# A second result row for each token's second expert, scatters without order, and gate/up weights read in 4 KB pieces

## The chip, the core and the metric

The kernel runs on one core of a Trainium2 chip. The metric is the device time of one execution in microseconds (us). Before the change it is 875.87 us, the median of 3 runs (875.46 to 876.12). The engines are TensorE (PE in the profile, its weight loads PEld), VectorE (DVE), ScalarE (ACT), GpSimd (POOL) and SyncE (SP), each with an in-order queue of its own. DMA engines move data between HBM and the on-chip memory; SP and POOL issue nearly all transfers here.

## The reference

One layer of a streaming encoder on 512 prompt tokens and 64 sample tokens, 576 rows of 1024 values. First comes a token mixer (sparse attention and a convolution branch), which the change does not touch. Then the part that matters:

```
h2  = x * (1 + sc2) + sh2
g   = argmax(h2 @ w_group + b_group)            # one group of four experts
top = the two best of the four experts of g;  w_top = softmax(their logits) * softmax weight of g
act = silu(gate) * up * w_top                   # gate, up = split(h2 @ w_gate_up[e])   1024 -> 2 x 256
y   = sum over the token's two experts of act @ w_down[e]                       #        256 -> 1024
x   = layer_norm(ALPHA * x + (1 + g2) * y, ln2_g, ln2_b)
```

Every token goes to exactly two of sixteen experts.

## The kernel before, in words

All 576 rows are routed first. Each expert's tokens are then gathered, pushed through the expert, and scattered back.

- `h2_d` in HBM holds the rows h2. `gather` (POOL, indirect DMA, line 1112) brings the up to 128 rows of one block into a tile `xg`, of which there are three. The work is 15 blocks: fixed experts, experts of the router's order, two heavy experts with two blocks each, and three blocks that hold two small experts of 64 rows each.
- `rows_in` (line 1127) turns a block: eight PE transposes. In each, 128 columns of `xg` are the stationary operand, and the identity moves past. The trace names the operands moving first, stationary second (`pxt<-ident,xg`).
- `gate_up` (lines 144 to 146, or 1145 for a pair) multiplies with the gate/up weights. These come in pieces of 256 rows of the 1024 x 512 matrix, four to an expert, loaded ahead by SP into a ring of 24 pieces (`load_gate_up`, line 1083). ACT and DVE split each piece into a high and a low part (lines 139 and 140). `hidden`, `turned` and `down` (lines 1150 to 1179) follow.
- `add_rows` (line 1186) scales the result on DVE, and POOL scatters it into `z_d` with an indirect DMA that adds to what is there (line 1190). A pair of small experts is scattered in two halves. `z_d` has one row for each token. It starts as the second norm's constant row (line 416, written early), and `ax_rows` (line 888) adds ALPHA * x to it by an accumulating DMA. Since both experts of a token add to one row, every scatter waits until the one before has landed.
- The block with an overflow part of a heavy expert takes its row numbers from a table in HBM: `table` scatters numbers and weights (POOL, line 1250), `place_ids` loads them back (line 1258) and DVE works out what the block needs (lines 1260 to 1262).
- After the blocks stands a loop for rows that found no place (line 1484). Its count is read at run time; here it is zero, but all engines meet at a barrier at its entry. Then five tiles of `z_d` are loaded (`zt`, line 1515), normalised (DVE lines 804, 1517, 1518; ACT lines 1505, 1507) and written out (line 1519).

In the expert part the order on PE, DVE and ACT is the order in which the code is written. POOL and SP are ordered by the scheduler.

Of the kernel before, what the change touches and what calls it, by code (L numbers as in the profile page):

```python
# [10 lines left out]
F32 = mybir.dt.float32  # L11
# [47 lines left out]
def encoder_step(ctx: ExitStack, tc: tile.TileContext, a, o):  # L59
# [3 lines left out]
    def scratch(name, shape, dt=F32):  # L63
        return nc.dram_tensor(name, shape, dt).ap()
# [4 lines left out]
    z_d = scratch("z_scr", (T, D))  # L69
# [46 lines left out]
    for j in range(2):  # L116
        G.iota(pay[:, :, j, 0], pattern=[[128, NT]], base=0, channel_multiplier=1)
# [298 lines left out]
    G.dma_start(z_d, dap(rows_d, 9 * D, [[0, T], [1, D]]))  # L416
# [394 lines left out]
    tok1 = late.tile([128, NT], F32, name="tok1", bufs=1)  # L811
    G.iota(tok1, pattern=[[128, NT]], base=1, channel_multiplier=1, allow_small_or_imprecise_dtypes=True)
# [71 lines left out]
    def ax_rows(t, behind):  # L884
        n = TS[t]
        with tc.issue_after(behind):
            (G if t > 1 else V).tensor_tensor(xn[t][0:n], xn[t][0:n], axr[0:n], op=OP.mult)
            ax_sums.append(G.dma_start(dap(z_d, t * 128 * D, [[D, n], [1, D]]), xn[t][0:n], accum_op=OP.add).ins)
# [10 lines left out]
    def route(t0, t1):  # L899
# [46 lines left out]
        V.tensor_tensor(vid, E, tok1[:, None, t0:t1, None].to_broadcast(full), op=OP.mult)  # L946
# [44 lines left out]

    ise = late.tile([128, NE], F32, name="ise", bufs=1)
    idt = late.tile([128, NE], I32, name="idt", bufs=1)
    sel = late.tile([128, 2, NE], F32, name="sel", bufs=1)

    def token_columns(src, e0, e1):
        V.tensor_scalar(ise[:, e0:e1], src, 0.0, float(OOB), op0=OP.is_equal, op1=OP.mult)
        last = V.scalar_tensor_tensor(idt[:, e0:e1], src, -1.0, ise[:, e0:e1], op0=OP.add, op1=OP.add).ins
        V.tensor_scalar(sel[:, 1, e0:e1], src, float(SEQ), None, op0=OP.is_gt)
        V.tensor_scalar(sel[:, 0, e0:e1], sel[:, 1, e0:e1], -1.0, 1.0, op0=OP.mult, op1=OP.add)  # L1000
        return last
# [67 lines left out]

    ring = []  # L1070
# [7 lines left out]
    def load_gate_up(e, c, dst, eng=SY):  # L1078
        if isinstance(e, int):
            src = dap(a["w_gate_up"], (e * D + 256 * c) * 512, [[512, 128], [128 * 512, 2], [1, 512]])  # L1080
        else:
            src = a["w_gate_up"][0, bass.ds(e, 1), 256 * c:256 * c + 256].rearrange("o (k p) n -> p (o k) n", p=128)
        return eng.dma_start(dst.rearrange("p (k n) -> p k n", k=2), src).ins
# [34 lines left out]
    def rows_in(b, whole=False):  # L1118
        x = xg[b % 3]
        xh, xl = xhl[:, b % 2, 0], xhl[:, b % 2, 1]  # L1120
        if whole:
            xwhole[b] = wp.tile([128, KT, 128], F32, name="xw", tag="whi", bufs=3)
        for q in range(2):
            pt = trp("pxt")
            for i in range(4):
                k = 4 * q + i
                PE.transpose(pt[:, 128 * i:128 * i + 128], x[:, 128 * k:128 * k + 128], ident)
            pv_ = pt.rearrange("p (k t) -> p k t", k=4)
            if whole:
# [126 lines left out]
    def place_ids(c, eng=SY):  # L1256
        ido = late.tile([128, 2], I32, name="ido", tag="ido", bufs=NPAIR)
        eng.dma_start(ido, ids_d.rearrange("(c p) d -> c p d", p=64)[bass.ds(c, 2)].rearrange("o p d -> (o p) d"))
        so = late.tile([128, 2], F32, name="so", tag="so", bufs=NPAIR)
# [3 lines left out]
        return [ido[:, 0:1]], ido.bitcast(F32)[:, 1:2], so[:, 0:1], so[:, 1:2]  # L1263

    def static_args(es):
        e = es[0]
        w = wsl[:, e:e + 1] if e < NFIX else cols[:, 1, e - NFIX:e - NFIX + 1]
        return [idt[:, i:i + 1] for i in es], w, sel[:, 0, e:e + 1], sel[:, 1, e:e + 1]
# [295 lines left out]
```

## Time and profile before

| | |
|---|---|
| median of 3 runs | 875.87 us |
| the profiled execution | 876.71 us, of which the profile's span is 875.0 us |
| granted TensorE clock | 0.952 of full speed |
| PE, DVE, ACT, POOL busy | 791.9, 640.5, 358.6, 143.6 us |
| gate/up loads on SP | 62 of 512 KB, median 8.5 us to landing |
| down loads on SP | 32 of 512 KB, median 10.6 us to landing |
| scatters into the result buffer | 16 + 2 (table rows) |

The span is what one execution shows from the first to the last instruction; the execution's own time is 1.7 us more. The profile's chain of work that ended last is 58% PE. A share of busy time is a mean over stages, so the stages are read from windows.

### The profile page before, as it was taken

The page shows a single profiled execution, that of the slowest core. Times are in us where ns is not written, and L with a number is a line of the kernel's source. Part 1 is how long each engine was busy: PE and PEld are TensorE (multiplying, and loading weights), DVE is VectorE, ACT ScalarE, POOL GpSimd, SP SyncE. Part 2 cuts the span into 40 slices and gives each one's busy share as a digit, 9 for nine tenths or more (in the row PEclk, how much of TensorE's full clock was granted, in tenths as well). Part 3 has the DMA queues.
Part 4 walks back from the last instruction along what each step waited for, and adds up shares of the span by engine and source line. Part 5 has one row for each costly group of instructions (what it writes and reads, how often), then busy time and mean ns, then how long its engine had stood idle before and what let it go on. Part 6 is the DMA issues. An engine that isn't in the chain of part 4 may idle for free.

```text
span 875.0 us, 13257 instructions
## 1 busy us (share of the span) xinstructions
PE 791.9 (90%) x4827; PEld 640.9 (73%) x4827; DVE 640.5 (73%) x1255; ACT 358.6 (41%) x654; POOL 143.6 (16%) x172
## 2 busy tenths in 40 slices
PE   4899999999999999999999999799947999999920
PEld 3788888887878879879899789788836667645400
DVE  1569999989999889988896425437797697555516
ACT  3243232324344335547743852222433564344205
POOL 2300000310200000000100001020257532322220
PEclk9999999999999999999999999899956999999975
DMA  9997664491423224232443105677597999799525
GB/s 289 342 352 254 204 201 126 120 246 56 148 75 89 83 75 115 89 100 62 135 127 106 54 1 194 224 214 260 116 273 242 346 348 316 200 335 386 149 46 201
DMA packets 108866, 159.70 MB, mean 183 GB/s; under 512 B 9715, under 2 KB 67211, under 8 KB 108801
## 3 DMA queue, kind: packets, MB, share of 16 engines
q1 hardware_dynamic: 94464, 120.38, 42.1%
q0 software_dynamic: 12736, 34.26, 15.3%
q10 hardware_dynamic: 1600, 4.22, 1.3%
q8 instruction: 38, 0.62, 0.3%
q14 instruction: 28, 0.22, 0.1%
HBM read 143.65 MB, written 26.13 MB: 194 GB/s over the span
## 4 chain that ended last, share of the span: by engine, by line
PE 58%; DVE 7%; DMA 7%; issue 2%; ACT 2%; POOL 1%; POOLq 0%; SPq 0%; DVEq 0%; ACTq 0%
PE acc L242 7%; PE acc L244 7%; PE acc L243 7%; PE pd L1175 4%; PE pdot L528 3%; PE pg L1145 2%; DMA wraw<-in_w_att_out_dram 2%; PE tm L144 2%; PE tm L146 2%; PE tm L145 2%; PE pl L652 2%; PE po L660 2%; PE pg L144 2%; DMA z_scr<-yo,idt 2%; PE pg L146 2%
## 5 line engine op out<-in xcount | busy, mean ns | idle before, releaser
L588 DVE SCALAR_TENSOR_TENSOR y<-ue,dwT,y 128x604 f32<-128x604 f32 (+17 forms) x232 | 183.2, 828 | 1.9 <-ACT y L586 1.5
L242 PE MATMUL acc<-hh,wlo 128*128 128x288 f32 (+1 forms) x504 | 152.7, 304 | 1.6 <-DVE wlo L140 1.6
L243 PE MATMUL acc<-hh,whi 128*128 128x288 f32 (+1 forms) x504 | 150.4, 299 | 0.0
L244 PE MATMUL acc<-hl,whi 128*128 128x288 f32 (+1 forms) x504 | 149.3, 300 | 0.0
L139 ACT CAST whi<-wraw 128x1024 fp32r<-128x1024 f32 (+1 forms) x72 | 75.0, 1043 | 172.7 <-PE acc L244 85.5
L140 DVE TENSOR_TENSOR wlo<-wraw,whi 128x1024 fp32r<-128x1024 f32 (+1 forms) x72 | 87.4, 1214 | 52.6 <-ACT whi L139 52.3
L242 PEld LDWEIGHTS acc<-hh,wlo 128*128 128x128 f32 (+1 forms) x504 | 94.2, 187 | 17.5 <-issue 8.8
L243 PEld LDWEIGHTS acc<-hh,whi 128*128 128x128 f32 (+1 forms) x504 | 94.2, 187 | 5.2 <-issue 5.1
L244 PEld LDWEIGHTS acc<-hl,whi 128*128 128x128 f32 (+1 forms) x504 | 93.7, 187 | 5.5 <-issue 5.2
L144 PE MATMUL tm<-wlo,hh 128*128 128x512 f32 x128 | 50.5, 397 | 0.4 <-DVE wlo L140 0.4
L145 PE MATMUL tm<-whi,hh 128*128 128x512 f32 x128 | 50.4, 393 | 0.0
L146 PE MATMUL tm<-whi,hl 128*128 128x512 f32 x128 | 49.8, 392 | 0.0
L140 DVE TENSOR_TENSOR wlo<-ring,whi 128x1024 fp32r<-128x1024 f32 x30 | 36.3, 1222 | 13.2 <-ACT whi L139 13.0
L1175 PE MATMUL pd<-ring,hT 128*128 128x512 f32 x96 | 44.5, 607 | 1.0 <-ACT hT L1159 1.0
L242 PE MATMUL acc<-oh,wlo 128*128 128x288 f32 x128 | 39.4, 308 | 5.6 <-DVE gt L744 5.1
L139 ACT CAST whi<-ring 128x1024 fp32r<-128x1024 f32 x30 | 31.3, 1049 | 29.0 <-PE pg L146 25.4
L244 PE MATMUL acc<-yl,whi 128*128 128x288 f32 x128 | 39.3, 310 | 0.6 <-DVE yl L721 0.5
L1190 POOL DMA_INDIRECT z_scr<-yo,idt x16 | 28.3, 1769 | 68.6 <-DMA z_scr<-yo,idt 29.8
L244 PE MATMUL acc<-ol,whi 128*128 128x288 f32 x128 | 39.2, 309 | 0.0
L243 PE MATMUL acc<-oh,whi 128*128 128x288 f32 x128 | 39.1, 306 | 0.0
L243 PE MATMUL acc<-yh,whi 128*128 128x288 f32 x128 | 38.3, 301 | 0.0
L242 PE MATMUL acc<-yh,wlo 128*128 128x288 f32 x128 | 37.9, 297 | 0.0
(474 smaller groups left out, 1769.0 us busy)
## 6 DMA issues: line engine op xcount, KB each, us to landing
ring<-in_w_gate_up_dram SPq DMA_DIRECT2D x62, 512.0 KB, 8.5
wraw<-in_w_in_dram SPq DMA_DIRECT2D x48, 512.0 KB, 4.9
wada<-in_w_ada_dram SPq DMA_DIRECT2D x32, 512.0 KB, 6.0
ring<-in_w_down_dram SPq DMA_DIRECT2D x32, 512.0 KB, 10.6
wada<-in_w_ada_dram SPq DMA_DIRECT2D x32, 256.0 KB, 6.2
gates_scr<-glg POOLq DMA_DIRECT2D x16, 288.0 KB, 2.6
gt<-gates_scr POOLq DMA_DIRECT2D x16, 288.0 KB, 3.1
wraw<-in_w_conv_out_dram SPq DMA_DIRECT2D x8, 512.0 KB, 4.0
```

Of the source, the lines that this page charges most:

```text
L139: split_copy[0] = S.copy(hi, raw).ins
L140: V.tensor_tensor(lo, raw, hi, op=OP.subtract)
L144: PE.matmul(out, lh, rl, start=start, stop=False)
L145: PE.matmul(out, lh, rh, start=False, stop=False)
L146: PE.matmul(out, ll, rh, start=False, stop=stop)
L242: PE.matmul(ps[h][0:m, 0:288], wl[:, k, :], xh[:, k, sl], start=k == 0, stop=False)
L243: PE.matmul(ps[h][0:m, 0:288], wh[:, k, :], xh[:, k, sl], start=False, stop=False)
L244: return PE.matmul(ps[h][0:m, 0:288], wh[:, k, :], xl[:, k, sl], start=False, stop=k == KT - 1).ins
L528: PE.matmul(pdt[0:n, 0:L], qiT[pr, h // 2, 128 * t:128 * t + n], kiT[pr, k0:k0 + L], start=True, stop=True)
L588: V.scalar_tensor_tensor(y[:, 30 - i:EXT], ue[:, 0:EXT - 30 + i], dwT[:, j, i:i + 1], y[:, 30 - i:EXT], op0=OP.mult, op1=OP.add)
L1175: PE.matmul(pd_[c], hT[:, k, :], dns[0][k][:, cs], start=k == 0, stop=k == 1)
L1190: sc = G.indirect_dma_start(out=z_d, out_offset=bass.IndirectOffsetOnAxis(ap=idx[0:128 // len(ids)], axis=0), in_=y[half], in_offset=None, ...
```

## The change

The result buffer gets two rows for each token, one for its first and one for its second expert. Row numbers of the second expert are the token's number plus 576. From them DVE works out a token number for the gather and keeps the raw number for the scatter. No two scatters write the same row, so they are declared independent. A pair's two halves go out in one scatter: 15 scatters in place of 18. The first half of the buffer is written by `ax_rows` without adding; only the second half starts as the constant row. At the end both rows of a token are loaded, and DVE adds them.

A gate/up piece now holds, for partition p, the matrix rows 8p + 2c and 8p + 2c + 1, which lie side by side in HBM: 4 KB in one stretch in place of two of 2 KB. To match, the transposes take columns k, k + 8, k + 16, ... of `xg` in place of 128 columns side by side.

```
-    z_d = scratch("z_scr", (T, D))
+    z_d = scratch("z_scr", (2 * T, D))
-        G.iota(pay[:, :, j, 0], pattern=[[128, NT]], base=0, channel_multiplier=1)
+        G.iota(pay[:, :, j, 0], pattern=[[128, NT]], base=j * T, channel_multiplier=1)
-    G.dma_start(z_d, dap(rows_d, 9 * D, [[0, T], [1, D]]))
+    G.dma_start(dap(z_d, T * D, [[D, T], [1, D]]), dap(rows_d, 9 * D, [[0, T], [1, D]]))
...
-            ax_sums.append(G.dma_start(dap(z_d, t * 128 * D, [[D, n], [1, D]]), xn[t][0:n], accum_op=OP.add).ins)
+            ax_sums.append(G.dma_start(dap(z_d, t * 128 * D, [[D, n], [1, D]]), xn[t][0:n]).ins)
...
     def token_columns(src, e0, e1):
+        V.tensor_scalar(second[:, e0:e1], src, float(T), -float(T), op0=OP.is_gt, op1=OP.mult)
         V.tensor_scalar(ise[:, e0:e1], src, 0.0, float(OOB), op0=OP.is_equal, op1=OP.mult)
-        last = V.scalar_tensor_tensor(idt[:, e0:e1], src, -1.0, ise[:, e0:e1], op0=OP.add, op1=OP.add).ins
-        V.tensor_scalar(sel[:, 1, e0:e1], src, float(SEQ), None, op0=OP.is_gt)
+        V.tensor_tensor(tok[:, e0:e1], second[:, e0:e1], src, op=OP.add)
+        last = V.scalar_tensor_tensor(idt[:, 0, e0:e1], tok[:, e0:e1], -1.0, ise[:, e0:e1], op0=OP.add, op1=OP.add).ins
+        V.scalar_tensor_tensor(idt[:, 1, e0:e1], src, -1.0, ise[:, e0:e1], op0=OP.add, op1=OP.add)
+        V.tensor_scalar(sel[:, 1, e0:e1], tok[:, e0:e1], float(SEQ), None, op0=OP.is_gt)
...
-            src = a["w_gate_up"][0, bass.ds(e, 1), 256 * c:256 * c + 256].rearrange("o (k p) n -> p (o k) n", p=128)
-        return eng.dma_start(dst.rearrange("p (k n) -> p k n", k=2), src).ins
+            src = a["w_gate_up"][0, bass.ds(e, 1)].rearrange("o (p k) n -> p (o k n)", p=128)[:, 1024 * c:1024 * c + 1024]
+        return eng.dma_start(dst, src).ins
...
-        x = xg[b % 3]
+        xk = xg[b % 3].rearrange("t (p k) -> t p k", k=KT)
...
-                PE.transpose(pt[:, 128 * i:128 * i + 128], x[:, 128 * k:128 * k + 128], ident)
+                PE.transpose(pt[:, 128 * i:128 * i + 128], xk[:, :, k], ident)
...
-        for i, idx in enumerate(ids):
-            half = slice(128 // len(ids) * i, 128 // len(ids) * (i + 1))
-            sc = G.indirect_dma_start(out=z_d, out_offset=bass.IndirectOffsetOnAxis(ap=idx[0:128 // len(ids)], axis=0),
-                                      in_=y[half], in_offset=None, bounds_check=T - 1, oob_is_err=False, compute_op=OP.add)
-        scatters.append(sc.ins)
+        sc = G.indirect_dma_start(out=z_d, out_offset=bass.IndirectOffsetOnAxis(ap=ids[1], axis=0), in_=y, in_offset=None,
+                                  bounds_check=2 * T - 1, oob_is_err=False, compute_op=OP.add).ins
+        for other in scatters:
+            tc.declare_no_dep(sc, other, reason="every row is written by one expert")
+        scatters.append(sc)
...
         V.tensor_copy(so[:, 0:1], ido[:, 0:1])
-        V.tensor_scalar(so[:, 1:2], so[:, 0:1], float(SEQ), None, op0=OP.is_ge)
+        V.tensor_scalar(so[:, 1:2], so[:, 0:1], float(T), -float(T), op0=OP.is_ge, op1=OP.mult)
+        V.tensor_tensor(so[:, 2:3], so[:, 0:1], so[:, 1:2], op=OP.add)
+        V.tensor_copy(idr, so[:, 2:3])
+        V.tensor_scalar(so[:, 1:2], so[:, 2:3], float(SEQ), None, op0=OP.is_ge)
...
-        zt = slot([128, D], name="zt")
-        SY.dma_start(zt[0:n], dap(z_d, t * 128 * D, [[D, n], [1, D]]))
+        z2 = slot([128, 2, D], name="zt")
+        SY.dma_start(z2[0:n], dap(z_d, t * 128 * D, [[D, n], [T * D, 2], [1, D]]))
+        zt = z2[:, 0, :]
+        V.tensor_tensor(zt[0:n], zt[0:n], z2[0:n, 1, :], op=OP.add)
```

Three places in the instruction order. On DVE, before the change, where the two table blocks get their row numbers (`so`) and the pairs theirs (`idt`), between two splits of weights:

```order
L140 TENSOR_TENSOR gs<-ring,gs 128x1024
L1260 CAST so<-ido 128x1
L1261 TENSOR_SCALAR so<-so 128x1
L1262 TENSOR_SCALAR so<-so 128x1
...
L997 TENSOR_SCALAR ise<-cols 128x6
L998 SCALAR_TENSOR_TENSOR idt<-cols,ise 128x6
L999 TENSOR_SCALAR sel<-cols 128x6
L1000 TENSOR_SCALAR sel<-sel 128x6
L140 TENSOR_TENSOR wlo<-ring,whi 128x1024 x2
```

The same place on DVE in the changed kernel (`idr` is the token number that the gather takes, `tok` the pairs' token number):

```order
L1267 CAST so<-ido 128x1
L1268 TENSOR_SCALAR so<-so 128x1
L1269 TENSOR_TENSOR so<-so 128x1
L1270 CAST idr<-so 128x1
L1271 TENSOR_SCALAR so<-so 128x1
L1272 TENSOR_SCALAR so<-so 128x1
...
L1000 TENSOR_SCALAR second<-cols 128x6
L1001 TENSOR_SCALAR ise<-cols 128x6
L1002 TENSOR_TENSOR tok<-second,cols 128x6
L1003 SCALAR_TENSOR_TENSOR idt<-tok,ise 128x6
L1004 SCALAR_TENSOR_TENSOR idt<-cols,ise 128x6
```

The rows up to the dots come twice in both, and two more for `sel` follow the last shown of the changed kernel: 19 small instructions stand where 10 stood, ahead of the same two splits.

On POOL, before the change, the end of the program from the last gather on; the nine scatters all stand ahead of the loop (L1484):

```order
L1112 DMA xg<-h_scr,idt 128x1024
L1190 DMA z_scr<-yo,idt 576x1024 x9
L1482 TENSOR_LOAD ovi
L1484 COMPARE_AND_BRANCH
L1484 ISA
L1484 UNCONDITIONAL_BRANCH
```

The end of POOL's program in the changed kernel, where the loop is L1494 and the dots stand for its barrier and its body:

```order
L1119 DMA xg<-h_scr,idt 128x1024
L1194 DMA z_scr<-yo,idt 1152x1024 x5
L1492 TENSOR_LOAD ovi
L1494 COMPARE_AND_BRANCH
L1494 ISA
L1494 UNCONDITIONAL_BRANCH
...
L1494 REGISTER_ALU
L1494 COMPARE_AND_BRANCH
L1494 UNCONDITIONAL_BRANCH
L1194 DMA z_scr<-yo,idt 1152x1024
```

Nine scatters have become six, and the last of them, that of the last block, stands behind the loop and its barrier.

On DVE, before the change, the first rows behind the loop, where the result tiles (`zt`) are normalised:

```order
L804 BN_STATS bs<-zt 128x6 x2
L806 BN_AGGR mv<-bs 128x2
L1517 SCALAR_TENSOR_TENSOR zt<-zt,mv,rows_7924 128x1024
L1506 TENSOR_SCALAR mv<-mv 128x1
L808 RECIPROCAL mv<-mv 128x1
```

The same place on DVE in the changed kernel:

```order
L1527 TENSOR_TENSOR zt<-zt 128x1024
L804 BN_STATS bs<-zt 128x6 x2
L806 BN_AGGR mv<-bs 128x2
L1529 SCALAR_TENSOR_TENSOR zt<-zt,mv,rows_7934 128x1024
L1527 TENSOR_TENSOR zt<-zt 128x1024
L808 RECIPROCAL mv<-mv 128x1
L1530 SCALAR_TENSOR_TENSOR zt<-zt,mv,rows_7934 128x1024
```

Each of the five tiles has an addition (L1527) that was not there, and the second tile's stands ahead of the first tile's reciprocal.

## Rows read from the trace of the kernel before

**Rows 1.** Windows: busy us by engine, granted clock, DMA share, GB/s.

```profile
704.00:813.50 109.50, 108.20 (x462) 63.83 (x463) 71.83 (x96) 50.20 (x72) 28.33 (x19) 1.00 0.95 318
813.50:837.00 23.50, 21.53 (x85) 10.49 (x83) 10.69 (x13) 7.04 (x11) 7.57 (x4) 1.00 0.34 85
837.00:855.00 18.00, 0.36 (x1) 0.00 (x0) 1.21 (x2) 0.00 (x0) 3.24 (x3) 0.65 0.37 85
855.00:875.00 20.00, 0.00 (x0) 0.00 (x0) 14.39 (x22) 11.88 (x22) 0.00 (x0) 0.50 0.50 184
```

**Rows 2.** Waits, 640 to 876 us: total us, times, longest.

```profile
POOL z_scr L1190 <- DMA z_scr<-yo,idt: 38.6, 7, 8.9
PE pxt L1127 <- DMA xg<-h_scr,idt: 5.2, 2, 3.3
```

**Rows 3.** Chain that ended last: start, us, link.

```profile
844.35 5.70 DMA z_scr<-yo,idt
850.70 3.76 DMA zt<-z_scr
```

**Rows 4.** Timeline of DVE, the last two blocks' results: start, us, instruction.

```profile
828.80 0.69 DVE L1186 TENSOR_TENSOR yo<-yo,pd 128x512 f32<-128x512 f32 x1 [0.60 <-PE pd L1179]
837.40 0.69 DVE L1186 TENSOR_TENSOR yo<-yo,pd 128x512 f32<-128x512 f32 x1 [0.63 <-PE pd L1175]
```

**Rows 5.** Timeline of POOL, three of the last four scatters.

```profile
828.23 1.57 POOL L1190 DMA_INDIRECT z_scr<-yo,idt  x1 [2.87 <-DVE yo L1186]
834.96 2.30 POOL L1190 DMA_INDIRECT z_scr<-yo,idt  x1 [5.17 <-DMA z_scr<-yo,idt]
840.14 1.41 POOL L1190 DMA_INDIRECT z_scr<-yo,idt  x1 [2.88 <-DMA z_scr<-yo,idt]
```

**Rows 6.** Line 1190, the scatters, issue to landing in us.

```profile
DMA to landing us min/median/max: 3.5/7.5/10.9
```

**Rows 7.** Line 1484, the loop's entry on DVE: ns each, first and last start.

```profile
L1484 DVEq EVENT_SEMAPHORE  x13: 21/50/4167, 839.1 to 850.7; - x13
```

**Rows 8.** Timeline of DVE, the normalisation at the end.

```profile
854.48 1.29 DVE L804 BATCH_NORM_STATS2 bs<-zt 128x6 f32<-128x512 f32 x2 [16.39 <-DMA zt<-z_scr]
858.56 0.16 DVE L808 RECIPROCAL mv<-mv 128x1 f32<-128x1 f32 x1 [1.16 <-ACT mv L807]
869.71 1.28 DVE L1518 SCALAR_TENSOR_TENSOR zt<-zt,mv,rows 64x1024 f32<-64x1024 f32 x1
```

**Rows 9.** Groups by form: DVE instructions; busy us, mean ns of one, idle before.

```profile
L843 DVE TENSOR_TENSOR h<-xn,rows 128x1024 f32<-128x1024 f32 x4 | 4.9, 1217 | 0.0
L780 DVE TENSOR_REDUCE bw<-wrs 128x20 f32<-128x160 f32 x2 | 0.9, 445 | 0.0
L1046 DVE TENSOR_REDUCE place<-M 128x12 f32<-128x144 f32 x1 | 0.3, 283 | 0.0
```

**Rows 10.** Windows of DMA: one us of result loads; 512-byte pieces; the last weights.

```profile
853.00:854.00 1.00, 0.00 (x0) 0.00 (x0) 0.00 (x0) 0.00 (x0) 0.00 (x0) 0.50 0.94 377
25.00:60.00 35.00, 32.08 (x339) 28.81 (x340) 18.23 (x41) 13.65 (x25) 6.09 (x13) 0.95 1.08 359
780.00:813.50 33.50, 33.50 (x153) 16.22 (x152) 18.85 (x21) 15.07 (x22) 7.22 (x5) 1.00 1.04 375
```

**Rows 11.** Timeline of DVE, first and last of the ten small instructions.

```profile
695.21 0.15 DVE L1260 CAST so<-ido 128x1 f32<-128x1 int32 x1 [5.34 <-DMA ido<-ids_scr]
696.57 0.41 DVE L1000 TENSOR_SCALAR sel<-sel 128x6 f32<-128x6 f32 x1
```

**Rows 12.** Timeline of PE, around two blocks' transposes.

```profile
704.38 0.44 PE L1157 MATMUL pht<-ident,hm 128*128 128x128 f32 x2 [0.54 <-DVE hm L1151]
714.71 1.04 PE L1127 MATMUL pxt<-ident,xg 128*128 128x128 f32 x8
715.59 1.45 PE L1175 MATMUL pd<-ring,hT 128*128 128x512 f32 x3
```

**Rows 13.** Tile xg: the transposes; ns min/median/max, first and last start.

```profile
L1127 PE MATMUL pxt<-ident,xg x120: 270/273/473, 667.5 to 814.2; 128*128 128x128 f32 x120
```

More of the change, by code (lines that the diff above doesn't have):

```diff
@@ L809, in stats @@
         return mv[0:n, 0:1], mv[0:n, 2:3]
-    tok1 = late.tile([128, NT], F32, name="tok1", bufs=1)
-    G.iota(tok1, pattern=[[128, NT]], base=1, channel_multiplier=1, allow_small_or_imprecise_dtypes=True)
+    tok1 = late.tile([128, 2, NT], F32, name="tok1", bufs=1)
+    G.iota(tok1, pattern=[[T, 2], [128, NT]], base=1, channel_multiplier=1, allow_small_or_imprecise_dtypes=True)
     iota128 = late.tile([128, 128], F32, name="iota128", bufs=1)
@@ L945, in route @@
         full = [128, 2, nt, 16]
-        V.tensor_tensor(vid, E, tok1[:, None, t0:t1, None].to_broadcast(full), op=OP.mult)
+        V.tensor_tensor(vid, E, tok1[:, :, t0:t1, None].to_broadcast(full), op=OP.mult)
         V.tensor_tensor(er, E, pr[:, 0:16 * nt].rearrange("p (t e) -> p t e", e=16)[:, None].to_broadcast(full), op=OP.mult)
@@ L992, in encoder_step @@
     ise = late.tile([128, NE], F32, name="ise", bufs=1)
-    idt = late.tile([128, NE], I32, name="idt", bufs=1)
+    second = late.tile([128, NE], F32, name="second", bufs=1)
+    tok = late.tile([128, NE], F32, name="tok", bufs=1)
+    idt = late.tile([128, 2, NE], I32, name="idt", bufs=1)
     sel = late.tile([128, 2, NE], F32, name="sel", bufs=1)
     def token_columns(src, e0, e1):
+        V.tensor_scalar(second[:, e0:e1], src, float(T), -float(T), op0=OP.is_gt, op1=OP.mult)
         V.tensor_scalar(ise[:, e0:e1], src, 0.0, float(OOB), op0=OP.is_equal, op1=OP.mult)
-        last = V.scalar_tensor_tensor(idt[:, e0:e1], src, -1.0, ise[:, e0:e1], op0=OP.add, op1=OP.add).ins
-        V.tensor_scalar(sel[:, 1, e0:e1], src, float(SEQ), None, op0=OP.is_gt)
+        V.tensor_tensor(tok[:, e0:e1], second[:, e0:e1], src, op=OP.add)
+        last = V.scalar_tensor_tensor(idt[:, 0, e0:e1], tok[:, e0:e1], -1.0, ise[:, e0:e1], op0=OP.add, op1=OP.add).ins
+        V.scalar_tensor_tensor(idt[:, 1, e0:e1], src, -1.0, ise[:, e0:e1], op0=OP.add, op1=OP.add)
+        V.tensor_scalar(sel[:, 1, e0:e1], tok[:, e0:e1], float(SEQ), None, op0=OP.is_gt)
         V.tensor_scalar(sel[:, 0, e0:e1], sel[:, 1, e0:e1], -1.0, 1.0, op0=OP.mult, op1=OP.add)
@@ L1079, in load_gate_up @@
         if isinstance(e, int):
-            src = dap(a["w_gate_up"], (e * D + 256 * c) * 512, [[512, 128], [128 * 512, 2], [1, 512]])
+            src = dap(a["w_gate_up"], (e * D + 2 * c) * 512, [[KT * 512, 128], [1, 1024]])
         else:
-            src = a["w_gate_up"][0, bass.ds(e, 1), 256 * c:256 * c + 256].rearrange("o (k p) n -> p (o k) n", p=128)
-        return eng.dma_start(dst.rearrange("p (k n) -> p k n", k=2), src).ins
+            src = a["w_gate_up"][0, bass.ds(e, 1)].rearrange("o (p k) n -> p (o k n)", p=128)[:, 1024 * c:1024 * c + 1024]
+        return eng.dma_start(dst, src).ins
     def load_down(e, k, dst):
@@ L1258, in place_ids @@
         eng.dma_start(ido, ids_d.rearrange("(c p) d -> c p d", p=64)[bass.ds(c, 2)].rearrange("o p d -> (o p) d"))
-        so = late.tile([128, 2], F32, name="so", tag="so", bufs=NPAIR)
+        so = late.tile([128, 3], F32, name="so", tag="so", bufs=NPAIR)
+        idr = late.tile([128, 1], I32, name="idr", tag="idr", bufs=NPAIR)
         V.tensor_copy(so[:, 0:1], ido[:, 0:1])
-        V.tensor_scalar(so[:, 1:2], so[:, 0:1], float(SEQ), None, op0=OP.is_ge)
+        V.tensor_scalar(so[:, 1:2], so[:, 0:1], float(T), -float(T), op0=OP.is_ge, op1=OP.mult)
+        V.tensor_tensor(so[:, 2:3], so[:, 0:1], so[:, 1:2], op=OP.add)
+        V.tensor_copy(idr, so[:, 2:3])
+        V.tensor_scalar(so[:, 1:2], so[:, 2:3], float(SEQ), None, op0=OP.is_ge)
         V.tensor_scalar(so[:, 0:1], so[:, 1:2], -1.0, 1.0, op0=OP.mult, op1=OP.add)
-        return [ido[:, 0:1]], ido.bitcast(F32)[:, 1:2], so[:, 0:1], so[:, 1:2]
+        return [idr, ido[:, 0:1]], ido.bitcast(F32)[:, 1:2], so[:, 0:1], so[:, 1:2]
     def static_args(es):
@@ L1267, in static_args @@
         w = wsl[:, e:e + 1] if e < NFIX else cols[:, 1, e - NFIX:e - NFIX + 1]
-        return [idt[:, i:i + 1] for i in es], w, sel[:, 0, e:e + 1], sel[:, 1, e:e + 1]
+        return [idt[:, i, e:e + 1] for i in range(2)], w, sel[:, 0, e:e + 1], sel[:, 1, e:e + 1]
     class Unit:
```

## The prediction
> **What bounds the kernel now.** I read the windows by stage first, since a mean over the span mixes stages, then the waits, then the end of the chain, then timelines at the places that the change touches. In the windows the reader is to see two stages [rows 1]. From 704 to 813.5 us PE is busy for 108.2 of 109.5 us at the full clock: PE sets the pace, and a microsecond more or less on PE there is one at the end. From 837 to 875 us PE has nothing to do; the end is scatters, result loads and normalisation, 38 us of 875.
>
> The waits say how much a better transfer can give [rows 2]. POOL waits 38.6 us for earlier scatters, but POOL's idle time counts only where something waits for POOL. PE waits for gathered rows twice, 5.2 us in total, longest 3.3; no wait of PE's matmuls for ring pieces stands in that view. The end of the chain shows where POOL's waiting does count: the last scatter starts at 844.35 and lands 5.70 later, and the first result tile, asked for at 850.70, lands 3.76 later [rows 3]. DVE had that scatter's rows ready at 837.40 + 0.69 = 838.1 [rows 4]. The scatter was late because three before it ran in turn, at 828.23, 834.96 and 840.14, two of them the halves of one pair [rows 5].
>
> **The change part by part.** All terms are against the profiled execution, 876.71 us (span 875.0 plus 1.7 around it), 0.84 above the median of the runs.
>
> *Scatters without order.* The last scatter no longer waits for those before. But it now stands behind the loop's barrier on POOL. DVE comes to that barrier at 839.1 [rows 7], after its last rows; SP waits there for the scatter before, whose rows are ready at 828.80 + 0.69 = 829.5 [rows 4], so with 5.7 us it lands near 835.5: DVE is the last to come. The kernel before leaves the loop and asks for results 0.65 us after its last landing (844.35 + 5.70 = 850.05, 850.70) [rows 3]; I take that as the barrier's price, plus 0.3 for POOL to start: scatter at 840.1, landing 845.8, result loads at 845.95 in place of 850.70. Term: -4.75. Its bounds are the shortest and longest landing, 3.5 and 10.9 us [rows 6]: -7.0 to +0.4. I take 5.7, since it is the same scatter with no weights left to load.
>
> *Two result rows to load.* The first tile is 1 MB in place of 512 KB. At 377 GB/s, the rate of these loads [rows 10], 512 KB more take 1.4 us; parts of later tiles come between, so up to 2.2. I take +1.75, with bounds 1.3 and 2.2. Later tiles land 2.8 us apart at that rate, faster than DVE uses them.
>
> *Five additions.* An f32 addition of two 128x1024 tiles takes 1.217 us on DVE [rows 9], five take 6.1. Nothing hides them: from 854.48 to the last instruction's end at 869.71 + 1.28 = 870.99, DVE is idle only for 1.16 us ahead of one reciprocal [rows 8]. The second tile's addition stands in just that gap. Going through the new order by hand, with ACT's two passes a tile beside it, ACT makes DVE wait again for about 0.9 us, as it gets each tile only after the addition. Term: 6.1 - 1.16 + 0.9 = +5.8; bounds 4.9 and 7. The last output write follows as before.
>
> *Row numbers on DVE.* Ten small instructions run from 695.21 until 696.65 [rows 11], 0.144 us each; nine more cost 1.3 us. They stand in DVE's queue ahead of two weight splits and the rows behind them, and PE already waits 0.54 us for DVE at 704.38 [rows 12], so nothing covers them there. Four more of the kind stand ahead of the first gather, for which PE waits; at most 0.144 each, and as three of them follow instructions that they need not wait for, 0.35 in all. Term: +1.65; bounds 0 (if PE comes later to that place for another reason, below) and 2.
>
> *Strided transposes.* The stationary operand of each transpose is 128 columns, 8 floats apart instead of side by side. No row shows PE reading so. What bounds it: eight transposes take from 714.71 to 715.59 [rows 12], 0.110 us each. The lower end is no change. The nearest rows are DVE's: a sum over 144 values side by side takes 283 ns, one over 160 values that lie 20 floats apart 445 ns [rows 9]. With 1.06 ns for a value side by side (the addition's 1217 ns against 283 ns, over 880 values more) and so 130 ns fixed, a value far apart costs (445 - 130)/160 = 1.97 ns, 1.86 times as much. If PE slows by that factor, a transpose takes 0.204 us, +0.75 a block; if the 1.97 ns themselves hold for its 128 columns, 0.252 us, +1.14 a block. There are 120/8 = 15 blocks [rows 13]; the first four come before 704 us, where PE waits for rows anyway, and eleven stand in the stretch where PE sets the pace. I take the factor: 11 x 0.75 = +8.3; bounds 0 and 11 x 1.14 + 1.1 = 13.6.
>
> [...]
>
> *4 KB pieces.* Transfers of 512-byte pieces run at 359 GB/s with the engines full, the weights of the last blocks, two thirds of them in 2 KB pieces, at 375 [rows 10]: piece size moves the rate little. And PE does not wait for the pieces. What hides them is the ring, four experts ahead; without that cover a late piece would cost PE its lateness. Term: 0. Bounds: a fuller or emptier DMA system moves the gathers and the table that share it. The second gather wait of PE is 5.2 - 3.3 = 1.9 us [rows 2], after which it may lose as much again at the lower clock: -3.8; I allow the same upward, +3.8, if a longer piece holds each engine longer against POOL's small ones.
>
> *The rest.* `ax_rows` no longer reads while it writes, and writes ahead of any scatter: 0. One gather moves ahead of the two table loads on POOL; it costs them at most its time on POOL, less than the shortest scatter's 1.41 us [rows 5], and as the table loads wait for the table to land there I take 0. The merged halves save POOL three issues of 1.4 to 2.3 us [rows 5], in idle time: 0.
>
> Sum: -4.75 + 1.75 + 5.8 + 1.65 + 8.3 = +12.75, so 889.5 for the profiled execution and 888.6 for the median.
>
> **The rivals.**
> 1. PE reads strided columns at its old rate. For it: weight loads may lie under the moving pass. Against it: DVE's rows. Then +4.45: 880.3 (877.7 to 883 with the other bounds).
> 2. Faster: the DMA system drains better, and POOL's transfers land near their shortest, 3.5 us [rows 6]. It decides if PE reads at its old rate and the gather at about 690 us lands 1.9 us sooner, before PE comes to it. Then PE saves 3.8, DVE's extra instructions run while it would have waited for the table (5.34 us [rows 11]), and the last scatter lands 2.2 sooner: -4.75 - 2.2 + 1.75 + 5.8 - 3.8 = -3.2, so 872.7. Against it: the rates of rows 10 hardly differ by piece.
> 3. The two halves of the end cancel: adds and loads cost what the scatters give back (bounds -7.0 + 1.3 + 4.9 = -0.8), transposes cost nothing, DVE's numbers 1: about 876.
> 4. The change does not do what it says: scatters still wait on each other. Then the term of -4.75 is gone, and the time is 893.4. The order against it: only one of POOL's last scatters waits for anything but its rows and a semaphore used eight transfers earlier.
>
> **How the numbers follow.** The forecast, transposes slowed, has 0.53; its own range is 884 to 893. Rival 1 has 0.27, rival 2 0.07, rival 3 0.10, rival 4 0.03. The predicted time is 888.6. The range runs from 876.5 to 893.5: it holds the forecast and rival 1 with their bounds, and leaves out rival 2 and parts of rivals 3 and 4. A measurement here tells 0.2% (1.75 us) from no change. Faster than that: rival 2 and a little of rival 3, 0.09; within it: 0.10; slower: 0.81.
>
> **What would show it.** The strided transposes: eight in a row, 0.88 us from first start to the next product now, should take near 1.6; if they still take 0.9, rival 1 holds. The end: the last scatter near 2 us after DVE's last result rows, with no wait for another scatter, but the gap from the first result tile's landing to the end should grow from 20.5 to about 26 us. DVE's small instructions behind the table load should take 2.7 us in place of 1.4. The forecast is wrong if PE's stretch of eleven blocks is not longer; it errs the other way if PE waits for ring pieces or gathers longer than now.

## The result and the profile after

The changed kernel takes 880.07 us against 876.0 for the kernel before (medians of 20 runs each). The ratio is 1.0058, 95% interval 1.0035 to 1.0080: slower, as forecast, but by 4.1 us and not by 12.7. The profiled executions agree: span 879.1 us against 875.0.

The windows of the changed kernel, the first as in [rows 1], the others cut at its own last rows and first landing (columns as there):

```profile
704.00:813.50 109.50, 108.37 (x463) 64.23 (x461) 72.48 (x97) 50.72 (x73) 27.86 (x19) 1.00 0.94 322
813.50:838.00 24.50, 22.53 (x88) 10.89 (x86) 10.69 (x13) 7.04 (x11) 3.11 (x2) 1.00 0.33 81
838.00:852.50 14.50, 0.12 (x1) 0.00 (x0) 0.70 (x2) 1.28 (x1) 1.55 (x1) 0.67 0.40 118
852.50:879.00 26.50, 0.00 (x0) 0.00 (x0) 20.57 (x27) 10.82 (x21) 0.00 (x0) 0.50 0.62 212
```

The stretch where PE sets the pace looks as before: 463 products where 462 were, in the same time. Most of what moved lies behind 838 us. Its two links in the chain of waits, against [rows 3] (start, us, link):

```profile
840.92 6.11 DMA z_scr<-yo,idt
847.05 5.42 DMA zt<-z_scr
```

The timeline of POOL, its last two scatters, against [rows 5] (start, us, instruction, in brackets the idle time before and what ended it):

```profile
830.54 1.55 POOL L1194 DMA_INDIRECT z_scr<-yo,idt  x1 [9.11 <-DVE yo L1193]
840.92 1.55 POOL L1194 DMA_INDIRECT z_scr<-yo,idt  x1 [8.83 <-issue]
```

And in the waits of 640 to 880 us, against [rows 2]:

```profile
POOL z_scr L1194 <- DVE yo L1193: 78.2, 13, 10.3
```

No scatter waits for another any more. The last one still starts 2.07 us after DVE's last rows (838.16 + 0.69 = 838.85), behind the loop's entry, and no semaphore ends that wait ("issue"). DVE's timeline, against [rows 4, 8]: the last result rows, the first two additions and the last instruction.

```profile
838.16 0.69 DVE L1193 TENSOR_TENSOR yo<-yo,pd 128x512 f32<-128x512 f32 x1 [0.63 <-PE pd L1182]
852.49 1.23 DVE L1527 TENSOR_TENSOR zt<-zt 128x1024 f32<-128x1024 f32 x1 [13.65 <-DMA zt<-z_scr]
856.51 1.22 DVE L1527 TENSOR_TENSOR zt<-zt 128x1024 f32<-128x1024 f32 x1
873.71 1.28 DVE L1530 SCALAR_TENSOR_TENSOR zt<-zt,mv,rows 64x1024 f32<-64x1024 f32 x1
```

DVE's timeline at the small instructions, the first of them and the split of weights behind the last, against [rows 11]: the 19 take 697.28 - 694.52 = 2.76 us where 10 took 1.44.

```profile
694.52 0.15 DVE L1267 CAST so<-ido 128x1 f32<-128x1 int32 x1
697.28 1.23 DVE L140 TENSOR_TENSOR wlo<-ring,whi 128x1024 fp32r<-128x1024 f32 x1
```

The transposes, as a view of tile xg (ns shortest, median, longest), against [rows 13], and the timeline of PE at the sixth block, against [rows 12]:

```profile
L1134 PEld LDWEIGHTS pxt<-ident,xg x120: 186/192/231, 666.1 to 814.8; 128*128 128x128 f32 x120
L1134 PE MATMUL pxt<-ident,xg x120: 270/274/482, 666.1 to 814.9; 128*128 128x128 f32 x120
```

```profile
715.35 1.05 PE L1134 MATMUL pxt<-ident,xg 128*128 128x128 f32 x8
716.24 2.31 PE L1182 MATMUL pd<-ring,hT 128*128 128x512 f32 x5
```

Eight strided transposes take 0.89 us from first start to the next product; eight contiguous ones took 0.88. That is the term that failed.

Ahead of 704 us PE's waits changed places. A row of the waits of 640 to 838 us, against [rows 2], and a wait of 3.14 us in PE's timeline:

```profile
PE pxt L1134 <- DMA xg<-h_scr,idt: 2.4, 1, 2.4
```

```profile
682.48 0.69 PE L1164 MATMUL pht<-ident,hm 128*128 128x128 f32 x2 [3.14 <-DMA ids_scr<-pay,slt]
```

PE waits 2.4 us for gathered rows in place of 5.2. But it waits 3.14 us ahead of a product with a block's hidden values (`hm`), which the profile puts down to the table's transfer; the longest wait of that product in the kernel before is 1.0.

Since runs of one kernel differ by up to 1.8% here (868 to 884 us for the kernel before), most of what follows is read from stretches of the profile, between events that every kernel has. Each entry is a difference of two starts or ends in a timeline, in us:

| kernel | rank product to sixth block | sixth block to last rows | last rows to result loads | loads to first landing | landing to DVE's end |
|---|---|---|---|---|---|
| before | 59.14 | 123.38 | 12.61 | 3.78 | 16.51 |
| after | 60.03 | 123.50 | 8.20 | 5.44 | 22.50 |
| weights alone (e1) | 65.22 | 123.63 | 14.09 | 3.87 | 16.50 |
| no additions (e3) | 60.81 | 123.50 | 8.44 | 5.72 | 18.01 |
| result rows alone (e4) | 60.33 | 123.33 | 8.43 | 5.33 | 22.50 |
| scatter ahead of loop (e7) | 61.73 | 123.49 | 7.45 | 5.21 | 22.50 |
| additions on POOL (e8) | 60.33 | 123.48 | 7.90 | 5.17 | 27.95 |
| small tile first (e11) | 60.27 | 123.50 | 7.33 | 6.22 | 22.32 |
| accumulating loads (e12) | 61.89 | 123.50 | 7.59 | 6.06 | 22.05 |

The first column is from PE's first rank product (655.57 before, 655.32 after) to the start of the transposes at 714.71 and 715.35. After against before: +0.89 + 0.12 - 4.41 + 1.66 + 5.99 = +4.25; with 0.25 less ahead of the rank product and 0.1 more behind DVE it is the 4.1 of the spans.

### The profile page after: what moved, and what is told of

It is laid out like the page before. It is cut to its first block, busy times and chain, and to the rows that moved or that the text cites. A ratio compares the mean times of both kernels' runs of the same rounds, so it can differ in the third digit from the quotient of the medians.

```text
span 879.1 us, 13265 instructions
## 1 busy us (share of the span) xinstructions
PE 792.4 (90%) x4827; PEld 641.6 (73%) x4827; DVE 647.6 (74%) x1275; ACT 358.5 (41%) x654; POOL 132.3 (15%) x169
## 4 chain that ended last, share of the span: by engine, by line
PE 60%; DVE 7%; DMA 4%; issue 2%; ACT 1%; POOL 1%; POOLq 0%; DVEq 0%; ACTq 0%
PE acc L242 7%; PE acc L244 7%; PE acc L243 7%; PE pd L1182 5%; PE pdot L528 3%; PE pg L1152 2%; PE pg L144 2%; DMA wraw<-in_w_att_out_dram 2%; PE pg L146 2%; PE pg L145 2%; PE tm L144 2%; PE tm L146 2%; PE tm L145 2%; PE pl L652 2%; PE po L660 2%
## 5 line engine op out<-in xcount | busy, mean ns | idle before, releaser
L1194 POOL DMA_INDIRECT z_scr<-yo,idt x13 | 22.3, 1712 | 83.2 <-DVE yo L1193 74.4
```

## The experiments

Theory: all of the 4.1 us comes from the result rows; strided transposes and 4 KB pieces cost nothing. Rivals: the transposes cost their 8 us and another part gave them back, or the end is bound by something else than the additions.

**The two halves of the change apart.** e1 is the kernel before with only the weight part:

```
-        x = xg[b % 3]
+        xk = xg[b % 3].rearrange("t (p k) -> t p k", k=KT)
-                PE.transpose(pt[:, 128 * i:128 * i + 128], x[:, 128 * k:128 * k + 128], ident)
+                PE.transpose(pt[:, 128 * i:128 * i + 128], xk[:, :, k], ident)
   (and load_gate_up as in the changed kernel)
```

> The kernel before with only the weight part of the change: gate/up pieces of 4 KB and strided transposes, one result row per token as before. Theory (strided transposes cost nothing because the longer weight load lies under the moving pass, and the pieces change nothing): ratio to before 1.000, within 0.3%; eight transposes 0.87 to 0.90 us, PE's waits for gathered rows as before, about 5 us. Rival (the transposes do cost about 8 us, but the pieces give it back in some other place, so that the two cancel): also about 1.000, but with eight transposes in 1.3 us or more. Second rival (4 KB pieces bring the gathers earlier, as the profile of the changed kernel had its first transposes 1.4 us earlier): 2 to 3 us faster, 0.997.

Measured: 877.17, ratio to before 1.0014 (0.9981 to 1.0046). The stretch of the last ten blocks is 123.63 us against 123.38, so the transposes cost next to nothing there, and nothing had to give their cost back. The profiled run lost 6 us in the first column: ACT waited ahead of the split of a ring piece, for something that the profile only calls "remote", and PE waited 8.2 us for the hidden values behind it. The same wait stands in the profile of e13 below, whose pieces are the old ones of 2 KB. ACT's timeline in e1, and in e13:

```profile
684.83 1.04 ACT L139 CAST whi<-ring 128x1024 fp32r<-128x1024 f32 x1 [5.16 <-remote]
```

```profile
686.37 1.04 ACT L139 CAST whi<-ring 128x1024 fp32r<-128x1024 f32 x1 [4.51 <-remote]
```

So it isn't the 4 KB pieces that make it. Both profiled executions are among the longest of their kernels (884.61 us with a median of 877.17, 885.58 with 878.67), so it seems to come and go; what ACT waits for was not settled.

e2 is the changed kernel with the two `transpose` lines of before.

> The changed kernel with contiguous transposes again, 4 KB pieces kept, so that the columns of a block no longer match its weights' rows (the gate/up products are not those of the reference; the amount of work is the same). Theory: weight loads of the transposes fall from 192 to 141 ns, matmuls stay at 270 to 274 ns, and the time stays that of the changed kernel, 880, within 0.3%. Rival (the strided transposes cost 8 us and the pieces gave it back): 872.

Measured: 879.45, ratio 1.003 (1.000 to 1.006); loads 142 ns, matmuls 278. That is the changed kernel's time, not 872. (The profile of this run has the granted clock at 0.95 through the expert part, so its stretches are not in the table.)

e4 is the changed kernel with `load_gate_up` and the transposes of before.

> The changed kernel with the weight part undone: 2 KB pieces in pairs and contiguous transposes, two result rows kept. Theory (all of the +4.1 us comes from the result rows): the time of the changed kernel, 880, ratio to before 1.005. Rival (the weight part costs or gives several us that another part hides): 2 us or more away from the changed kernel.

Measured: 878.96, ratio 1.0058 (1.0024 to 1.0092), the changed kernel's own ratio. Its tile xg:

```profile
L1134 PEld LDWEIGHTS pxt<-ident,xg x120: 138/141/231, 661.0 to 809.9; 128*128 128x128 f32 x120
L1134 PE MATMUL pxt<-ident,xg x120: 270/273/474, 661.0 to 810.0; 128*128 128x128 f32 x120
```

The stride makes the record of a weight load longer, 192 in place of 141 ns, and leaves the matmul at 274 against 273. The table gives the price: 123.33 and 123.38 us with contiguous transposes, 123.48 to 123.63 with strided ones, so 0.1 to 0.3 us for ten blocks where 7.5 were forecast.

**Why the stride is free.** The first guess was that the longer load lies under the pass of the identity. e5 and e6 do each transpose as four products of 32 moving columns:

```
-                PE.transpose(pt[:, 128 * i:128 * i + 128], xk[:, :, k], ident)
+                for m in range(4):
+                    s = slice(32 * m, 32 * m + 32)
+                    PE.matmul(pt[:, 128 * i:128 * i + 128][:, s], xk[:, :, k], ident[:, s], start=True, stop=True)
```

> The changed kernel with each strided transpose cut into four of 32 moving columns, so that its 128-column weight load is done four times, with only a quarter of the moving pass to hide it: 32 pairs of load and matmul a block in place of 8; the result is the same. Compared with the same cut on contiguous columns (the next run). Theory (the stride makes the load itself longer, 192 in place of 141 ns, and only the moving pass of 110 ns hides it): a block's 32 take clearly longer strided than contiguous, by the ratio of the loads or 192/141 = 1.36 at most; PE is then bound by loads, 0.11 to 0.19 us each, 3.5 to 6.1 us a block. Rival (the longer record is only a longer way through the engine, and loads follow each other at the old rate): the same time per block in both, so that no moving pass is needed to hide anything.

> The same cut into four passes of 32 columns on contiguous transposes with 2 KB pieces; the result is the same. It is the measure for the run before: a block's 32 pairs take 32 times the rate of a contiguous load. If the load is hidden under the moving pass at 0.110 us, that rate is at most 0.110 us, so up to 3.5 us a block. Theory: less time a block than strided; rival: the same.

Measured: 1113.5 strided and 1024.0 contiguous, one run each. A pair here is one load of the stationary operand and one pass of the moving one. A block has 64 pairs in the trace and not 32: an ordinary f32 product is two pairs. Timelines of PE, a strided block (e5), then a contiguous one (e6) with the product behind it:

```profile
704.89 15.34 PE L1136 MATMUL pxt<-ident,xg 128*128 128x32 f32 x64
720.05 6.51 PE L1184 MATMUL pd<-ring,hT 128*128 128x512 f32 x8
```

```profile
715.46 8.22 PE L1136 MATMUL pxt<-ident,xg 128*128 128x32 f32 x64
723.49 6.07 PE L1184 MATMUL pd<-ring,hT 128*128 128x512 f32 x8
```

That is 0.237 us a pair against 0.125. But the granted clock stood at 0.62 and 0.87 in these two stretches, so by themselves they do not tell the load from the clock. e9 and e10 keep the full pass of 128 columns and use ordinary products (strided, and contiguous on e4's base):

```
-                PE.transpose(pt[:, 128 * i:128 * i + 128], xk[:, :, k], ident)
+                PE.matmul(pt[:, 128 * i:128 * i + 128], xk[:, :, k], ident, start=True, stop=True)
```

> The changed kernel with its transposes done as ordinary f32 products with the identity, 128 moving columns each, on the strided columns: the profile of the short passes showed that each such product is two pairs of load and pass, so a block has 16 pairs, each with a load of 128 strided columns and a full pass to hide it. The result is the same. In the short passes the granted clock was at 0.62 (strided) and 0.87 (contiguous) in the stretch that was compared, so they did not tell the load from the clock; full passes should keep the clock at 1.0. Theory (a strided load lies under a full pass): 16 x 0.110 = 1.76 us a block, as with contiguous columns (the next run). Rival (a strided load goes on at the 0.240 us of the short passes, and only the transpose's own mode of loading spares it): 16 x 0.240 = 3.8 us a block, 22 us more over eleven blocks.

> The same ordinary products with the identity on contiguous columns and 2 KB pieces; the result is the same. [...] Theory: strided within 0.1 us a block of this; rival: strided about twice this.

Measured: 918.4 and 889.4 us, one run each, with the granted clock at 1.00 from 700 to 830 us in both. Tile xg of e9, and of e10:

```profile
L1134 PEld LDWEIGHTS pxt<-ident,xg x240: 312/336/340, 664.4 to 852.5; 128*128 128x128 f32 x120
L1134 PE MATMUL pxt<-ident,xg x240: 274/402/606, 664.4 to 852.7; 128*128 128x128 f32 x120
```

```profile
L1134 PEld LDWEIGHTS pxt<-ident,xg x240: 186/192/338, 661.0 to 823.6; 128*128 128x128 f32 x120
L1134 PE MATMUL pxt<-ident,xg x240: 270/275/582, 661.0 to 823.7; 128*128 128x128 f32 x120
```

And one block of each in PE's timeline, with the product behind it:

```profile
724.26 3.97 PE L1134 MATMUL pxt<-ident,xg 128*128 128x128 f32 x16
728.06 3.60 PE L1182 MATMUL pd<-ring,hT 128*128 128x512 f32 x8
```

```profile
715.16 1.95 PE L1134 MATMUL pxt<-ident,xg 128*128 128x128 f32 x16
716.95 3.60 PE L1182 MATMUL pd<-ring,hT 128*128 128x512 f32 x8
```

The first guess fell. Strided, 16 pairs take 3.80 us, 0.238 each; contiguous 1.79, 0.112 each. The first block of each ran at half clock, 16 pairs as well, and its window tells the load from the clock (e9, then e10; columns as in [rows 1]):

```profile
664.44:668.28 3.84, 3.84 (x16) 3.84 (x17) 2.07 (x12) 0.59 (x1) 2.97 (x3) 0.50 0.76 162
```

```profile
660.96:664.40 3.44, 3.44 (x17) 3.44 (x17) 1.73 (x11) 0.59 (x1) 2.74 (x3) 0.50 0.89 158
```

Contiguous pairs follow the clock, 0.215 us at 0.50 and 0.112 at 1.00. Strided ones do not, 0.240 and 0.238. So the strided load sets the pace of an ordinary product, and neither a longer pass (0.237 us with 32 columns in e5, 0.238 with 128) nor a faster clock shortens it. In a transpose the same load goes at 0.111 us in the block shown, and at 0.099 to 0.124 in the blocks of the changed kernel at full clock; contiguous in e4 it is 0.098 to 0.121. So it is the transpose that is spared: one pair in place of two, and a load that the stride makes 1.36 times as long in the record and not measurably longer in the pace. Why a transpose's load is spared stays open, and whether it would show under a shorter pass was not tried.

**The additions.** e3 leaves them out.

```
-        V.tensor_tensor(zt[0:n], zt[0:n], z2[0:n, 1, :], op=OP.add)
```

> The changed kernel without the five additions at the end: both rows are loaded, but only the first is normalised, so the second expert's part is missing from the output. Theory (the additions are 6.0 of the +4.1 us): 880.1 - 6.0 = 874, about 2 below the kernel before. From the first result tile's landing to the end 20.5 in place of 26.6 us. Rival (the end is bound by the doubled loads, and the additions only fill their gaps): no more than 2 us less, 878 or above, with DVE waiting for tiles.

Measured: 876.02, ratio 1.0004 (0.9974 to 1.0035), and 18.01 us from first landing to DVE's end. The additions are 4.49 of the 5.99 us. The other 1.5 stand with the doubled loads: in e3 ACT has to wait for the second tile until 853.80, 2.6 us after the first landed, where before it had begun on it 1.3 us after. The start of DVE, that of ACT on the second tile and the last instruction in e3, and ACT's start on the second tile in the kernel before:

```profile
851.22 1.29 DVE L804 BATCH_NORM_STATS2 bs<-zt 128x6 f32<-128x512 f32 x2 [14.16 <-DMA zt<-z_scr]
853.80 1.06 ACT L1515 ACTIVATE jk<-zt 128x1024 f32<-128x1024 f32 x1 [0.72 <-DMA zt<-z_scr]
867.95 1.28 DVE L1529 SCALAR_TENSOR_TENSOR zt<-zt,mv,rows 64x1024 f32<-64x1024 f32 x1
```

```profile
855.77 1.06 ACT L1505 ACTIVATE jk<-zt 128x1024 f32<-128x1024 f32 x1 [21.11 <-DVE bs L804]
```

e8 gives four of them to POOL (`(G if t else V).tensor_tensor(...)`).

> The changed kernel with four of the five additions on POOL (the first tile's stays on DVE). An addition of this shape takes POOL 2.5 to 2.7 us, of which there is room for one a tile, as tiles come 2.8 us apart. Theory (the additions cost because they stand in DVE's queue): from the first landing to DVE's end 22.5 - 4 x 1.22 + up to 1.5 for tiles that come later = 18 to 19.5 us; 877. Rival (the loads of two rows bind the end, or POOL and DVE slow each other): 21 us or more, with DVE's own instructions longer than 1.28 us.

Measured: 885.47, ratio 1.0165 (1.0128 to 1.0203). The rival holds. DVE and POOL at 854 to 860 us, and SP, in that kernel's timeline:

```profile
854.73 3.22 DVE L1529 SCALAR_TENSOR_TENSOR zt<-zt,mv,rows 128x1024 f32<-128x1024 f32 x1
857.04 3.10 POOL L1527 TENSOR_TENSOR zt<-zt 128x1024 f32<-128x1024 f32 x1 [0.17 <-DMA zt<-z_scr]
861.65 1.33 SPq L1525 DMA_DIRECT2D zt<-z_scr  x2
```

DVE's instruction of 1.28 us takes 3.22 while POOL adds, and the next one 3.17; a later one (868.16), which began 0.08 us ahead of POOL's next addition, took 1.28. Besides, the scheduler put the last two loads behind the first output write, 15 us later than the first three, and the chain that ended last runs through them (861.65, 6.52 us to the landing). So e8 does not show what POOL's additions would cost with all five loads in time.

**The last scatter.** e7 puts it ahead of the loop.

```
+    with tc.issue_after(scatters[-1]):
         nvals = nc.values_load_multi_w_load_instructions(...)
```

> The changed kernel with the last scatter put ahead of the loop in POOL's queue. Theory (the loop's entry costs the last scatter most of the 2.07 us between DVE's last rows and its start, but the result loads then leave the loop only 0.65 us after the landing): scatter 0.1 to 0.3 us after the rows, result loads at rows + 0.2 + 6.1 + 0.65, 1.2 us sooner: 878.9, too little for the medians, to be read from the stretch between DVE's last rows and the result loads (8.2 us before, 7.0 forecast). Rival (the loop's barrier takes its 2 us whether the scatter lies ahead or behind): 8.2 us or more.

Measured: 879.55, ratio 1.0101 (1.0065 to 1.0136). The kernel before stood at 870.2 in that set of runs, which is where the ratio comes from; the kernel's own median is that of the changed one, within the scatter. In the profile the scatter starts 0.28 us after the last rows (839.23):

```profile
839.51 1.55 POOL L1194 DMA_INDIRECT z_scr<-yo,idt  x1 [7.03 <-DVE yo L1193]
846.68 2.96 SPq L1526 DMA_DIRECT2D zt<-z_scr  x5
```

From last rows to loads: 7.45 us against 8.20, 0.75 of the 1.2 forecast: the loads now leave the loop 0.94 us after the landing (839.51 + 6.23 = 845.74), where they followed it by 0.02 in the changed kernel and 0.65 was forecast.

**Other ways to load.** e11 adds to that the tile of 64 rows as the first (`for t in (4, 0, 1, 2, 3)`).

> The changed kernel with the last scatter ahead of the loop and the result tile of 64 rows taken first instead of last. Theory (the first load's landing grows with its size, 3.76 us for 512 KB and 5.42 for 1 MB): landing 3.8 us after it is asked for, 1.6 sooner; the additions stay, DVE's pace with them, so the whole is 1.6 plus the 0.75 of the scatter better than the changed kernel: 877.7. Rival (the second tile, now 1 MB, is what DVE waits for): landing sooner, but a wait of 1 us or more in front of the second tile, and no better than the scatter alone, 879.3.

Measured: 878.86, ratio 1.0045 (1.0012 to 1.0078). Neither came out: half the bytes land later, 6.22 us after they are asked for. Windows of e11, 1.5 us while the small tile comes and 2 us while the next does (columns as in [rows 10]), and in a fence of its own 4 us of the changed kernel's tiles of 128 rows:

```profile
849.66:851.16 1.50, 0.00 (x0) 0.00 (x0) 0.00 (x0) 0.00 (x0) 0.00 (x0) 0.50 1.01 199
852.66:854.66 2.00, 0.00 (x0) 0.00 (x0) 1.91 (x4) 0.00 (x0) 0.00 (x0) 0.50 1.04 416
```

```profile
850.05:854.05 4.00, 0.00 (x0) 0.00 (x0) 1.53 (x2) 0.00 (x0) 0.00 (x0) 0.50 1.03 420
```

With the DMA engines full in both, a tile on 64 partitions comes at 199 GB/s and one on 128 at 416 to 420. By an estimate from these rates its 512 KB take 2.6 us and 1 MB on 128 partitions 2.5, so it was the wrong test for the size of a load. The rate is not all of the later landing: 2 us after the loads were asked for, e11 still moved only 8 GB/s (847.66 to 848.66) and the changed kernel 270 (849 to 850). Why the small tile starts later was not settled.

e12 has POOL's accumulating transfers add the second rows of the last three tiles:

```
+            SY.dma_start(zt[0:n], dap(z_d, t * 128 * D, [[D, n], [1, D]]))
+            G.dma_start(zt[0:n], dap(z_d, (T + t * 128) * D, [[D, n], [1, D]]), accum_op=OP.add)
```

> As the run before, and the second rows of tiles 2 to 4 in order are added by POOL's accumulating transfers in place of DVE: three additions fewer, each with a second transfer behind the tile's first. Theory (additions are in DVE's queue and nowhere else late; the transfers lie under the work on the first two tiles): from the first landing to DVE's end 18 to 19.5 us, 3 x 1.2 less than the run before; 874, at or a little below the kernel before. Rival (the accumulating transfers land late, as they start only after the first rows' landing, and rob DVE or the loads): DVE or ACT waits for tiles, and the time is that of the run before or longer.

Measured: 876.93, ratio 1.0032 (1.0002 to 1.0061); 22.05 us from first landing to DVE's end against 22.32 in e11. Three additions fewer, and most of the time is given back, in part in ACT's waits for the transfers:

```profile
864.45 1.06 ACT L1516 ACTIVATE jk<-zt 128x1024 f32<-128x1024 f32 x1 [1.11 <-DMA zt<-z_scr]
868.82 1.06 ACT L1516 ACTIVATE jk<-zt 128x1024 f32<-128x1024 f32 x1 [1.44 <-DMA zt<-z_scr]
```

**Could the scatters' gain be had without the second row?** e13 and e14 are the kernel before with another order of blocks.

```
-    for kind in "mhhsmsmsm":
+    for kind in "mhshsmsmm":      # e13;  e14: "mhhssmsmm"
```

> The kernel before (one result row per token, ordered scatters) with only the order of the blocks changed: the last pair comes third from the end in place of second, and another pair between the two heavy experts. Theory (the last scatter was late because a pair's two scatters stood right before it, not because scatters wait on each other as such): the last scatter starts 0.3 to 1 us after DVE's last rows in place of 6.3, result loads at 0.65 after its landing, so up to 5.5 us less at the end: 869.5 to 871, if PE does not wait more for the pairs' weights. Rival (the scatters have a backlog all along, 6 to 8 us each under the weight loads): the last one still starts 3 us or more behind the rows, and the gain is 3 us or less, 872 or above.

> The kernel before with the first two pairs next to each other behind the heavy experts and two single experts at the end. Same theory for the end as in the run before: last scatter 0.3 to 1 us after the rows. It differs in the middle: two pairs in a row need four experts' weights at once, so PE should wait for ring pieces there, some us; 870 to 876. If PE does not wait, it ties with the run before.

Measured: e13 878.67, ratio 1.0017 (0.9988 to 1.0046); e14 885.94, ratio 1.0084 (1.0051 to 1.0116). Neither is faster. The rival of e13 holds. Its last two scatters in the chain that ended last (start, us, link; the dots are pieces left out); the rows of the last block are ready at 845.22 + 0.69 = 845.91:

```profile
846.11 5.99 DMA z_scr<-yo,idt
...
852.84 6.11 DMA z_scr<-yo,idt
```

The last scatter starts 6.9 us behind its rows with two single experts at the end as well. The one ahead of it had rows ready since 836.80 + 0.69 = 837.49 and started at 846.11: the scatters have a backlog, and work it off one landing at a time.

The last five blocks are the same in e14, and there the last scatter is on time, as was expected of it. Timelines of DVE, POOL and SP in its profile, which is of the longest of its twelve executions (894.12 us):

```profile
859.94 0.69 DVE L1186 TENSOR_TENSOR yo<-yo,pd 128x512 f32<-128x512 f32 x1 [0.63 <-PE pd L1175]
861.02 1.57 POOL L1190 DMA_INDIRECT z_scr<-yo,idt  x1 [5.17 <-DVE yo L1186]
868.07 2.36 SPq L1515 DMA_DIRECT2D zt<-z_scr  x5
```

The scatter starts 0.39 us behind its rows (860.63), and the result loads 7.44 us behind them, where the kernel before takes 12.61 and the changed one 8.20. So a scatter that has to wait for the one before need not be late: it is late where the ones before it are. In the kernel before they are, and there the second row buys 4.4 us; it costs 7.7 at the other end. In e14 the way from the sixth block to the last rows took 137.36 us in place of 123.38; whether the scatters caught up only because of that was not tried. e14 is 8.5 us above the kernel before at the median; where it loses them was not settled. No version tried beats the kernel before.

## Why the prediction was wrong

The direction was right, and the size was wrong by one step: **strided transposes**, forecast at +8.3 and measured at +0.12 in ten of the eleven blocks. "PE slows by that factor" carried a price from DVE's reads over to PE's load. The runs show that the price exists on PE, for ordinary products: 0.238 us a load against 0.112, a factor of 2.1, near the 0.252 us of the other bound. A transpose doesn't pay it (0.111 us against 0.110). The nearest row was of another engine, and not of the operation. The lower bound, 0, was what came, and rival 1 with its 880.3 is the case that happened: its reason was "weight loads may lie under the moving pass", and that reason fell too, since in an ordinary product the same pass hides nothing (e9, 0.238 us a pair, and e5, 0.237 with a quarter of the pass). That 880.3 is so near 880.07 is in part luck: 0.8 too much for the row numbers nearly makes up for the 0.6 by which the other terms together were short.

The other steps, by their terms:

- *Scatters without order*, -4.75: measured -4.41 relative to the last rows. The scatter started 2.07 us after the rows, as forecast (2.0), and landed in 6.11 in place of 5.7. In e13 the scatters before made the last one late again; e14 shows that ordered scatters need not.
- *Two result rows to load*, +1.75: +1.66 for the first tile. But the loads also brought the second tile later, which shows only without the additions (e3).
- *Five additions*, +5.8: +5.99, of which 4.49 go with the additions; the other 1.5 stand with the loads. The working was 6.1 less 1.16 plus 0.9; the gap ahead of the reciprocal was filled as described (856.51).
- *Row numbers on DVE*, +1.65: the 19 instructions took 1.32 us more, 1.3 forecast; the whole way to the sixth block took 0.89 more, and 1.13 to 2.75 in e3, e4, e7, e8, e11 and e12. That stretch holds other waits too, and varies by more than that (e1: 65.22), so the term is only known to be about 1 to 3.
- *4 KB pieces*, 0: e1, e2 and e4 show no difference at their medians' resolution of about 0.3%. Rival 2's time did not come, though its condition came in part: PE's waits for gathered rows fell from 5.2 to 2.4 us, and in e4, with 2 KB pieces, to 2.4 as well, so it isn't the pieces that did it. The changed kernel lost the gain again in the wait of 3.14 us at 682.48, where the prediction had none. The lower clock that its bound of 3.8 allowed for is in the trace of the kernel before: 0.71 from 692.13 to 698.00 us, behind the second wait for gathered rows.

Added up: 12.75 forecast, 8.2 of it too much for the transposes and 0.8 for the row numbers; the rest agrees within 0.4 a term.

## What to carry to other kernels

A price taken from DVE's strided reads, 1.86 times by the estimate from [rows 9], did not hold for PE's transposes: ask first in which form of the operation an engine loads. A transpose took 128 columns at a stride of 8 floats at its full pace (0.111 us against 0.110 side by side), an ordinary f32 product at less than half (0.238 against 0.112). And when a wait is bought off by splitting a buffer, price the merge where it will stand: here it stands behind the last landing, where nothing that was tried could hide it: POOL, accumulating transfers and another order of tiles did not make the whole faster than the kernel before.

## What the runs showed of the hardware

- An ordinary f32 product with the identity is two pairs of load and pass in the trace (x240 for 120), a transpose one; 16 contiguous pairs took 1.79 us (e10) and 8 transposes 0.88 (the kernel before).
- An ordinary product's pair with a strided f32 load took 0.240 us at a granted clock of 0.50 and 0.238 at 1.00 (e9): its pace did not follow the clock. A contiguous one took 0.215 and 0.112 (e10).
- While POOL added two 128x1024 tiles, DVE's instructions of 1.28 us took 3.2; one that began 0.08 us ahead of an addition of POOL's took 1.28 (e8).
- With the DMA engines full, a load on 64 partitions ran at 199 GB/s (e11), one on 128 partitions at 416 (e11) to 420 (the changed kernel).
